# Forming the state weights of a chunked state-space scan in turned layout, from planes repeated over partitions

## The chip, the cores and the metric

The kernel runs on one core of a Trainium2 chip. The time is the device time of one execution in microseconds; times of several executions are given as their median. TensorE is called PE, VectorE DVE, ScalarE ACT, GpSimd POOL and SyncE SP, as in the profile.

## The reference

One hybrid decoder layer on 512 positions of width 1024, all in float32:

```
h    = rms_norm(x) * norm_w
proj = h @ w_in        # u_s, z_s (1024 each), q, k, v (1536 each), z_a (512), r_s, r_a (1024 each)
y_s  = s5(u_s) * silu(z_s) @ w_ssm_out
y_a  = dilated_attention(rope(qknorm(q)), rope(qknorm(k)), v) * silu(z_a) @ w_attn_out
out  = x + (sigmoid(r_s) * y_s + sigmoid(r_a) * y_a) @ w_o
```

The change lies in the S5 branch. It has 64 groups of 16 channels with 64 complex states each:

```
A    = exp(lam * exp(log_dt))                  # per group g and state n, complex
f    = (A - 1) / lam
bb   = f * (b_re + i b_im)                     # (g, n, q): q is one of 16 channels
h_t  = A * h_{t-1} + bb . u_t                  # a scan over 512 positions
y_t  = Re(c . h_t) + d * u_t, then GELU and a gated linear unit with w_glu
```

## The kernel before

The sequence is cut into 64 chunks of T = 8 positions. For each chunk the 8 inputs of a group enter the state at the chunk's end with the weights W[(k, q), n] = bb[n, q] A[n]^(7-k), a matrix with 128 rows (8 positions x 16 channels) for each group's 64 states, real and imaginary part. Groups are taken in pairs; unit j (0 to 7) has 8 groups, that is 4 pairs. The stages:

- **Projection.** cm_unit makes a 128-column block of the projection: 24 matmuls of 128x512 (three per 128 rows, since each float32 factor is split into a high and a low part). The weights come in by SP's queue (w_raw, two buffers), ACT makes the high part w_hi (L250), DVE the low part w_lo (L252); each has three buffers.
- **Constants.** DVE computes A and f on 64 partitions (one per group) in scr; pw holds A^1 to A^8 and f, made by doubling (L555 to L558). PE turns f (f_turn, "ftp") and the powers (a_turn, "atp") so that the states lie on partitions: fT and AT. POOL and DVE form BB = f b (L587 to L590).
- **W units.** w_unit(j) forms on DVE, by coef (L422 to L424), the products BB A^k with the states on partitions: six operations of 128x512. PE turns them by eight transposes of 128x128 ("wps") and ACT copies them out as W (L447), two buffers.
- **X units.** x_unit(j) multiplies W with u of all chunks on PE ("xps"); u has been stored to DRAM and loaded back with (position, channel) on partitions (ud, Uj, and sza in which early loads are kept). ACT puts the result into Xs.
- **Scan.** DVE runs the scan over the chunks on Xs (step, run_end, run_carry; L746 to L769), and each output chunk(j) then multiplies Xs and M on PE ("yps").

PE's order is written out by hand: each projection block has four slots, and the list events says at which slot a piece of the S5 work is put between the projection's matmuls. wx(j) stands at slot 16 + 3j and holds w_unit(j) and x_unit(j - 1); the first output chunk stands at slot 88. The orders of the other engines are set by a scheduler when the program is built, from data dependencies. SP's queue is served in order: a DMA that waits for a buffer holds up those behind it. A tile's tag names the memory that it shares in turn with others.

The tile names that the rows use: dd holds b (D1), BB and later M; ab holds the products of coef, later the coefficients of the outputs (ca); scn is the scan's work space; pj is a projection's PSUM tile; th a gate.

Of the kernel before, what the change touches and what calls it, by code (L numbers as in the profile page):

```python
# [20 lines left out]
P = 128  # L21
# [31 lines left out]
def tile_hybrid_block(ctx: ExitStack, tc: tile.TileContext, x, positions, norm_w, w_in, lam_re, lam_im,  # L53
# [3 lines left out]
    act, dve, pool, sp = nc.scalar, nc.vector, nc.gpsimd, nc.sync  # L57
# [50 lines left out]
    def bank(name):  # L108
        return ps_tile("g", name)
# [4 lines left out]
    def t2k(name, dtype=F32):  # L114
        return tmp.tile([P, 512], dtype, name=name, tag="t2k")
# [290 lines left out]
    def load_u(j, Uj=None):  # L406
        if Uj is None:
            Uj = t2k("Uj")
        sp.dma_start(Uj, ud[j].rearrange("q g s c -> s q g c"))
        return Uj.rearrange("p (g c) -> p g c", g=8)  # L410
# [3 lines left out]
    def coef(dst, p0, a1, a2, n0, n1, t, eng):  # L414

        n, ng = n1 - n0, dst.shape[1]
        sh = [P, ng, n, Q]
        gs = slice(p0, p0 + ng)
        ar = AT[:, 0, gs, n0:n1].unsqueeze(3).broadcast_to(sh)
        ai = AT[:, 1, gs, n0:n1].unsqueeze(3).broadcast_to(sh)  # L420
        tv = t[:, 0:ng * n * Q].rearrange("p (g k q) -> p g k q", g=ng, k=n)
        dve.tensor_tensor(dst, a1.unsqueeze(2).broadcast_to(sh), ar, op=ALU.mult)  # L422
        eng.tensor_tensor(tv, a2.unsqueeze(2).broadcast_to(sh), ai, op=ALU.mult)
        coefs[0] = dve.tensor_tensor(dst, dst, tv, op=ALU.add).ins  # L424
# [3 lines left out]
    def u_unit(j, at=(), ps=None):  # L428
# [5 lines left out]
                               ps.rearrange("p (r j i h) -> p r j i h", r=4, h=2, i=NI)).ins)  # L434
        sp.dma_start(ud[j].rearrange("q g s c -> g q (s c)"), uT)

    def w_unit(j):
        ba = ab[j % 2][:, 0:8 * T * Q].rearrange("p (a g k q) -> p a g k q", a=2, g=4, k=T)
        p4 = slice(4 * j, 4 * j + 4)
        for a in range(2):  # L440
            coef(ba[:, a], 4 * j, BB[:, 1 + a, p4], BB[:, a, p4], 1, T + 1, ab[2][:, 512 * a:], dve)
        W = big.tile([P, 8, P], F32, name="W", tag=("s6a", "s6b")[j % 2])
        for h in range(2):
            ps = bank("wps")
            for g in range(4):
                pe.transpose(ps[:, g * P:(g + 1) * P], ba[:, h, g].rearrange("p k q -> p (k q)"), ident)
            act.copy(W[:, 4 * h:4 * h + 4].rearrange("p g n -> p (g n)"), ps)  # L447
# [71 lines left out]
    mag = scr([G, N])  # L519
# [4 lines left out]
    sn = scr([G, N])  # L524
    cs = scr([G, N])
    sincos(sn, cs, th_, [G, N], "la")

    pw = big.tile([G, 2, 9, N], F32, name="pw", tag="s7a")
    dve.tensor_tensor(pw[:, 0, 0], mag, cs, op=ALU.mult)
    dve.tensor_tensor(pw[:, 1, 0], mag, sn, op=ALU.mult)  # L530
    den = scr([G, N])
    nr = scr([G, N])
    t1 = scr([G, N])
    t2 = scr([G, N])
# [12 lines left out]
    dve.tensor_tensor(pw[:, 1, 8], t1, den, op=ALU.mult)
    tq = big.tile([G, 2, 4, N], F32, name="tq", tag="s7b")
    for n in (1, 2, 4):

        br_ = pw[:, 0:1, n - 1:n, :].broadcast_to([G, 2, n, N])
        bi_ = pw[:, 1:2, n - 1:n, :].broadcast_to([G, 2, n, N])
        a = pw[:, :, 0:n, :]
        o = pw[:, :, n:2 * n, :]
        dve.tensor_tensor(o, a, br_, op=ALU.mult)  # L555
        dve.tensor_tensor(tq[:, :, 0:n], a, bi_, op=ALU.mult)
        dve.tensor_tensor(o[:, 0], o[:, 0], tq[:, 1, 0:n], op=ALU.subtract)
        dve.tensor_tensor(o[:, 1], o[:, 1], tq[:, 0, 0:n], op=ALU.add)  # L558
# [17 lines left out]
    abt = big.tile([P, 4096], F32, name="ab", tag="s5")  # L576
    ab = [abt[:, i * nca:(i + 1) * nca] for i in range(3)]
    fr, fi = (fT[:, i:i + 1, :].unsqueeze(3).broadcast_to([P, 2, H, Q]) for i in range(2))
    tb = ab[0][:, 0:1024].rearrange("p (a g q) -> p a g q", a=2, g=H)
    def f_turn():  # L580
        pf = bank("ftp")
        for i in range(2):
            for h in range(2):
                pe.matmul(pf[64 * h:64 * h + 64, i * H:(i + 1) * H], pw[:, i, 8], idg[:, h], start=True, stop=True,
                          skip_group_check=True)
        act.copy(fT.rearrange("p a g -> p (a g)"), pf[:, 0:2 * H])
        pool.tensor_tensor(tb, D1, fi, op=ALU.mult)  # L587
        dve.tensor_tensor(BB[:, 1:3], D1, fr, op=ALU.mult)
        dve.tensor_tensor(BB[:, 2], BB[:, 2], tb[:, 0], op=ALU.add)
        dve.tensor_tensor(BB[:, 1], BB[:, 1], tb[:, 1], op=ALU.subtract)  # L590
        act.activation(BB[:, 0], BB[:, 2], AF.Copy, scale=-1.0)

    def a_turn():
        ps = bank("atp")
        for i in range(2):
            for k in range(8):
                for h in range(2):
                    o = i * 8 * H + (7 - k) * H
                    pe.matmul(ps[64 * h:64 * h + 64, o:o + H], pw[:, i, k], idg[:, h], start=True, stop=True,
                              skip_group_check=True)  # L600
        for i in range(2):
            act.copy(AT[:, i, :, 0:8], ps[:, i * 8 * H:(i + 1) * 8 * H].rearrange("p (k g) -> p g k", k=8))
# [120 lines left out]
    H = G // 2  # L723
# [215 lines left out]
    events = [(3, begin_x), (6, lambda: early.update({3: load_u(3, sza[:, 3])})), (8, f_turn), (10, a_turn)]  # L939
# [309 lines left out]
    for c in range(KT):  # L1249
# [5 lines left out]
        ps = cm_unit(gT_hi, gT_lo, at=[(2, turn_wcol)] if c == 1 else ())  # L1255
# [82 lines left out]
    for cc in range(KT // 2):  # L1338
# [8 lines left out]
        for c2 in range(2):  # L1347
            c = 2 * cc + c2
# [47 lines left out]
```

## Time and profile before

| | |
|---|---|
| median of 3 runs | 678.64 us (677.83 to 680.23) |
| the profiled execution | 678.55 us, its span 676.5 us |
| granted PE clock | 1.00 |
| PE busy | 669.5 us (99%) |
| DVE busy | 465.3 us (69%) |
| ACT busy | 322.5 us (48%) |
| POOL busy | 118.2 us (17%) |

Busy time of an engine is the time in which at least one of its instructions runs. A row of a timeline has the start from the span's beginning, the duration, the engine, the line of the kernel, the operation, output and inputs and the tile; "x2" marks two such in a row, taken together. Durations of successive operations of one engine overlap a little, so starts are a better measure of what a row of them takes. The page's chain of work that ended last is followed back from the end, at each step to what released it. A window's row has from:to, its length, the busy time of the engine asked for (and its instructions), then the granted clock, the mean busy share of the 16 DMA engines and the GB/s that they moved; where no engine's busy time is shown, SP was asked for. A row of waits has who waited for whom, the sum in us, how many times, and the longest.

### The profile page before, as it was taken

How to read it: one execution, taken by the hardware profiler on the slowest of the kernel's cores; microseconds unless marked ns; L12 is line 12 of the kernel's file. 1: busy time of each engine (PE TensorE's matmuls, PEld its weight loads, DVE VectorE, ACT ScalarE, POOL GpSimd, SP SyncE). 2: the span in 40 equal slices, each digit the busy share in tenths (PEclk: the TensorE clock that was granted, in tenths of full speed). 3: DMA queues.
4: the chain of work that ended last, by engine and by line, in shares of the span. 5: the costliest groups of instructions: out<-in, count | busy, mean ns of one | idle time of the engine just before them, and what ended most of it. 6: DMA issues, size and time to landing. Idle time of an engine off the chain costs nothing.

```text
span 676.5 us, 12719 instructions
## 1 busy us (share of the span) xinstructions
PE 669.5 (99%) x4841; PEld 565.3 (84%) x4841; DVE 465.3 (69%) x964; ACT 322.5 (48%) x677; POOL 118.2 (17%) x274
## 2 busy tenths in 40 slices
PE   8999999999999999999999999999999999999997
PEld 7988888889888888878889888888888888888886
DVE  7989879999788365863238777658566856667531
ACT  6644552423467663431344674557456745633210
POOL 1020000600365329510000030012001200220000
PEclk9999999999999999999999999999999999999999
DMA  9665425552566543573332423222222213237231
GB/s 307 134 164 146 122 55 146 148 167 85 156 141 147 148 148 107 155 249 94 93 107 81 140 63 95 62 63 74 84 83 74 72 55 94 94 134 286 94 125 62
DMA packets 137380, 82.13 MB, mean 121 GB/s; under 512 B 32736, under 2 KB 125928, under 8 KB 137192
## 3 DMA queue, kind: packets, MB, share of 16 engines
q1 hardware_dynamic: 134968, 78.31, 39.2%
q0 software_dynamic: 2048, 2.36, 2.2%
q8 instruction: 38, 0.62, 0.4%
q10 hardware_dynamic: 304, 0.66, 0.3%
q14 instruction: 22, 0.18, 0.1%
HBM read 68.46 MB, written 10.49 MB: 117 GB/s over the span
## 4 chain that ended last, share of the span: by engine, by line
PE 92%; DVE 4%; issue 2%; ACT 1%; DMA 1%; POOL 0%; ACTq 0%; DVEq 0%; POOLq 0%
PE pj L69 76%; PE sps L69 3%; PE yps L69 2%; PE ot L69 2%; PE ptp L74 2%; PE qtp L74 2%; PE xps L69 1%; DVE gth L1258 1%; DVE w_lo L252 1%; PE wps L74 1%; ACT w_hi L250 1%; DMA x_all<-in_x_dram 1%; PE kps L69 1%; PE yT L74 1%; PE cps L69 0%
## 5 line engine op out<-in xcount | busy, mean ns | idle before, releaser
L250 ACT ACTIVATE w_hi<-w_raw 128x1024 fp32r<-128x1024 f32 x94 | 99.4, 1059 | 162.0 <-PE pj L69 132.2
L252 DVE TENSOR_TENSOR w_lo<-w_raw,w_hi 128x1024 fp32r<-128x1024 f32 x94 | 117.1, 1247 | 66.3 <-ACT w_hi L250 65.3
L69 PE MATMUL pj<-hT_hi,w_hi 128*128 128x512 f32 (+1 forms) x344 | 131.8, 385 | 0.0
L69 PE MATMUL pj<-hT_lo,w_hi 128*128 128x512 f32 (+1 forms) x344 | 128.8, 376 | 0.4 <-DVE hT_lo L355 0.4
L69 PE MATMUL pj<-hT_hi,w_lo 128*128 128x512 f32 (+1 forms) x344 | 126.8, 375 | 0.0
L69 PE MATMUL pj<-w_hi,hT_hi 128*128 128x512 f32 (+1 forms) x288 | 108.7, 377 | 0.0
L69 PE MATMUL pj<-w_hi,hT_lo 128*128 128x512 f32 (+1 forms) x288 | 105.6, 367 | 0.0
L69 PE MATMUL pj<-w_lo,hT_hi 128*128 128x512 f32 (+1 forms) x288 | 105.5, 366 | 0.0
L69 PEld LDWEIGHTS pj<-hT_hi,w_hi 128*128 128x128 f32 x344 | 64.7, 188 | 13.1 <-issue 1.3
L69 PEld LDWEIGHTS pj<-hT_lo,w_hi 128*128 128x128 f32 x344 | 64.8, 188 | 11.1 <-DVE hT_lo L355 0.6
L69 PEld LDWEIGHTS pj<-hT_hi,w_lo 128*128 128x128 f32 x344 | 63.7, 188 | 12.0
L69 PEld LDWEIGHTS pj<-w_hi,hT_lo 128*128 128x128 f32 x288 | 54.3, 189 | 9.1
L69 PEld LDWEIGHTS pj<-w_hi,hT_hi 128*128 128x128 f32 x288 | 54.4, 189 | 8.5 <-issue 0.5
L69 PEld LDWEIGHTS pj<-w_lo,hT_hi 128*128 128x128 f32 x288 | 54.5, 189 | 7.5
L1120 POOL COPY sw<-st 32x4 f32<-32x4 f32 x64 | 11.9, 185 | 175.0 <-ACT Pt L1076 172.2
L1021 DVE SCALAR_TENSOR_TENSOR qkp<-qtp,wcol,qkp 128x512 fp32r<-128x512 f32 (+1 forms) x32 | 23.6, 748 | 25.3 <-ACT qkp L1020 25.2
L1076 ACT ACTIVATE Pt<-Pt,st 128x256 f32<-128x256 f32 (+1 forms) x64 | 30.9, 484 | 19.8 <-DVE st L1074 19.8
L845 POOL DMA_DIRECT2D dd<-kt x64 | 33.8, 536 | 2.4 <-POOL kt L841 2.1
L1020 ACT ACTIVATE qkp<-qtp,wcol 128x512 fp32r<-128x512 f32 (+1 forms) x32 | 21.2, 683 | 23.0 <-PE qtp L74 20.8
L69 PE MATMUL pj<-w_lo,mT_hi 128*128 128x512 f32 (+1 forms) x72 | 26.3, 366 | 0.0
L69 PE MATMUL pj<-w_hi,mT_hi 128*128 128x512 f32 (+1 forms) x72 | 26.3, 366 | 0.0
L69 PE MATMUL pj<-w_hi,mT_lo 128*128 128x512 f32 (+1 forms) x72 | 26.3, 365 | 0.0
(301 smaller groups left out, 1189.6 us busy)
## 6 DMA issues: line engine op xcount, KB each, us to landing
w_raw<-in_w_in_dram SPq DMA_DIRECT2D x36, 512.0 KB
w_raw<-in_w_in_dram SPq DMA_DIRECT2D x112, 128.0 KB
w_raw<-in_w_glu_dram SPq DMA_DIRECT2D x8, 512.0 KB
w_raw<-in_w_ssm_out_dram SPq DMA_DIRECT2D x8, 512.0 KB
w_raw<-in_w_o_dram SPq DMA_DIRECT2D x8, 512.0 KB
w_early<-in_w_in_dram SPq DMA_DIRECT2D x4, 512.0 KB
ud<-uT SPq DMA_DIRECT2D x8, 256.0 KB
uss<-ud SPq DMA_DIRECT2D x8, 256.0 KB
```

The source lines that it names most:

```text
L69: last[0] = nc.tensor.matmul(*a, **k)
L74: last[0] = nc.tensor.transpose(*a, **k)
L250: last_act[0] = act.activation(hi, raw, AF.Copy).ins
L252: dve.tensor_tensor(lo, raw, hi.bitcast(F32), op=ALU.subtract)
L845: pool.dma_start(M[Q * t:Q * t + Q, :, 0:P - Q * t], kt[:, :, t:].rearrange("q g k p -> q g (k p)"))
L1020: act.activation(hi, ps[sl], AF.Copy, scale=w)
L1021: dve.scalar_tensor_tensor(lo, ps[sl], w, hi.bitcast(F32), op0=ALU.mult, op1=ALU.subtract)
L1076: act.activation(o, o, AF.Exp, bias=nm, scale=-1.0, accum_out=st[:, kind, 1, h, b:b + 1])
L1120: pool.tensor_copy(sw[32 * r:32 * r + 32, :, :, b], st[32 * b:32 * b + 32, 1, :, :, r])
L1258: dve.scalar_tensor_tensor(th, th, 1.0, z, op0=ALU.add, op1=ALU.mult)
```

## The change

The weights W are formed at once in the layout that x_unit needs, with (k, q) on partitions, so that PE need not turn them. For this the factors are laid out by DMA:

- **pf**: on 64 partitions (one per group) DVE forms f A^(7-k) for k = 0 to 7, from the powers A^1 to A^7 (three doublings, the last of three powers) and f. It is stored to DRAM as pfd.
- **btd**: b is turned once by eight transposes (b_turn, "btp", slot 4), copied by ACT and stored to DRAM by eight DMAs.
- **load_planes(j)**: four DMAs bring unit j's planes to 128 partitions x 512: pfd with each k's row repeated over the 16 channels, btd with each channel's row repeated over the 8 positions, real and imaginary part of each. Units 0 and 1 are loaded at slot 11; unit j + 2 is loaded when w_unit(j) has used its planes. The planes lie in ab's memory, two sets.
- **w_unit(j)**: the complex product of the planes, two multiplications of 128x1024, a subtraction and an addition of 128x512, written to W. No transposes, no copies by ACT.
- **f_turn** turns f and A; **a_powers** (slot 12) makes A^2 to A^8 on DVE from the turned A, with the states on partitions, in place of a_turn's 32 calls on PE. The copy of BB with its sign turned goes.

```diff
+    def load_planes(j):
+        PB = planes[j % 2].rearrange("p (a c) -> p a c", a=4)
+        for i in range(2):
+            p_, b_ = pfd[i, :, 8 * j], btd[i, :, 4 * j]
+            sp.dma_start(PB[:, i], bass.AP(p_.tensor, p_.offset, [(G * N, T), (0, Q), (1, 512)]))
+            sp.dma_start(PB[:, 2 + i], bass.AP(b_.tensor, b_.offset, [(0, T), (G * N, Q), (1, 512)]))
+        PBs[j] = PB
+
     def w_unit(j):
-        ba = ab[j % 2][:, 0:8 * T * Q].rearrange("p (a g k q) -> p a g k q", a=2, g=4, k=T)
-        p4 = slice(4 * j, 4 * j + 4)
-        for a in range(2):
-            coef(ba[:, a], 4 * j, BB[:, 1 + a, p4], BB[:, a, p4], 1, T + 1, ab[2][:, 512 * a:], dve)
+        PB = PBs.pop(j)
         W = big.tile([P, 8, P], F32, name="W", tag=("s6a", "s6b")[j % 2])
-        for h in range(2):
-            ps = bank("wps")
-            for g in range(4):
-                pe.transpose(ps[:, g * P:(g + 1) * P], ba[:, h, g].rearrange("p k q -> p (k q)"), ident)
-            act.copy(W[:, 4 * h:4 * h + 4].rearrange("p g n -> p (g n)"), ps)
+        Wv = W.rearrange("p (a m) n -> p a (m n)", a=2)
+        br, bi = (PB[:, 2 + i].unsqueeze(1).broadcast_to([P, 2, 512]) for i in range(2))
+        dve.tensor_tensor(Wv, PB[:, 0:2], br, op=ALU.mult)                      # L451
+        dve.tensor_tensor(PB[:, 0:2], PB[:, 0:2], bi, op=ALU.mult)              # L452
+        dve.tensor_tensor(Wv[:, 0], Wv[:, 0], PB[:, 1], op=ALU.subtract)        # L453
+        dve.tensor_tensor(Wv[:, 1], Wv[:, 1], PB[:, 0], op=ALU.add)             # L454
+        if j + 2 < 8:
+            load_planes(j + 2)
         return W
...
+    def times(o, a, br_, bi_, t):                                               # L562 to L565
+        dve.tensor_tensor(o, a, br_, op=ALU.mult)
+        dve.tensor_tensor(t, a, bi_, op=ALU.mult)
+        dve.tensor_tensor(o[:, 0], o[:, 0], t[:, 1], op=ALU.subtract)
+        dve.tensor_tensor(o[:, 1], o[:, 1], t[:, 0], op=ALU.add)
+
+    for n, m in ((1, 1), (2, 2), (4, 3)):
+        e = T - 1
+        sh = [G, 2, m, N]
+        times(pw[:, :, e - n - m:e - n], pw[:, :, e - m:e], ...)
+    sh = [G, 2, T - 1, N]
+    times(pf[:, :, 0:T - 1], pw[:, :, 0:T - 1], f1[:, 0:1]..., f1[:, 1:2]..., tq)
+    pfd = dram.tile([2, T, G, N], F32, name="pfd")
+    sp.dma_start(pfd.rearrange("a k g n -> g (a k) n"), pf.rearrange("g a k n -> g (a k) n"))
...
+    def b_turn():
+        bt = dd[:, 2048:3072].rearrange("p (a m c) -> p a m c", a=2, m=4)
+        for i in range(2):
+            ps = bank("btp")
+            for m in range(4):
+                pe.transpose(ps[:, m * P:(m + 1) * P], D1[:, i, 8 * m:8 * m + 8]..., ident)
+            act.copy(bt[:, i].rearrange("p m c -> p (m c)"), ps)
+            for m in range(4):
+                sp.dma_start(btd[i, :, 8 * m:8 * m + 8].rearrange("q m c -> m q c"), bt[:, i, m])
...
-    def a_turn():
-        ...                                    # 32 calls of pe.matmul into "atp", two copies to AT
+    def a_powers():
+        tv = t2k("tv")[:, 0:8 * H].rearrange("p (a g k) -> p a g k", a=2, g=H)
+        for n in (1, 2, 4):
+            sh = [P, 2, H, n]
+            times(AT[:, :, :, T - 2 * n:T - n], AT[:, :, :, T - n:T], ...)
...
-    events = [(3, begin_x), (6, ...), (8, f_turn), (10, a_turn)]
+    events = [(3, begin_x), (6, ...), (4, b_turn), (8, f_turn), (12, a_powers)]
+    events += [(11, lambda: load_planes(0)), (11, lambda: load_planes(1))]
```

On DVE, between the making of BB and the second X unit, the order before has the products of coef (L422 to L424, six per unit, all written to ab) with the low parts of weights between them:

```order
L422 TENSOR_TENSOR ab_518<-dd_513,AT_508 128x512 x4
L423 TENSOR_TENSOR ab_518<-dd_513,AT_508 128x512 x2
L252 TENSOR_TENSOR w_lo_692<-w_raw_689,w_hi_691 128x1024
L424 TENSOR_TENSOR ab_518<-ab_518 128x512 x2
```

On DVE at the same place now, W_748, W_775 and W_833 are the weights of units 0, 1 and 2, and ab holds the planes:

```order
L451 TENSOR_TENSOR W_748<-ab_525 128x1024
L451 TENSOR_TENSOR W_775<-ab_525 128x1024
L452 TENSOR_TENSOR ab_525<-ab_525 128x1024 x2
L453 TENSOR_TENSOR W_748<-W_748,ab_525 128x512
L454 TENSOR_TENSOR W_748<-W_748,ab_525 128x512
L252 TENSOR_TENSOR w_lo_744<-w_raw_741,w_hi_743 128x1024
L453 TENSOR_TENSOR W_775<-W_775,ab_525 128x512
L454 TENSOR_TENSOR W_775<-W_775,ab_525 128x512
L451 TENSOR_TENSOR W_833<-ab_525 128x1024
```

Units 0 and 1 run interleaved, and unit 2's first product, which needs new planes, follows the last of unit 1 at once.

On SP's queue, from the store of u's block 4 (uT_602) on, before:

```order
L435 DMA ud_336<-uT_602 8x16x512
L210 DMA w_raw_723<-in_w_in_dram 128x8x128
L435 DMA ud_336<-uT_686 8x16x512
L210 DMA w_raw_816<-in_w_in_dram 128x8x128
L435 DMA ud_336<-uT_720 8x16x512
```

On SP's queue from the store of the same block (uT_630 in the changed program) on, now:

```order
L435 DMA ud_336<-uT_630 8x16x512
L577 DMA pfd_513<-pf_480 64x16x64
L443 DMA ab_525<-btd_526 128x1x512 x4
L210 DMA w_raw_690<-in_w_in_dram 128x8x128
L442 DMA ab_525<-pfd_513 128x1x512 x4
L435 DMA ud_336<-uT_687 8x16x512
L210 DMA w_raw_741<-in_w_in_dram 128x8x128
L435 DMA ud_336<-uT_738 8x16x512
L210 DMA w_raw_814<-in_w_in_dram 128x8x128
L443 DMA ab_525<-btd_526 128x1x512 x4
L442 DMA ab_525<-pfd_513 128x1x512 x2
L210 DMA w_raw_878<-in_w_in_dram 128x8x128
```

The planes of units 0 and 1 (the first rows with ab) and then those of unit 2 stand between the weights and the stores of u; a plane that waits for DVE to finish with ab holds up the weights behind it. On PE the eight groups wps and the group atp are gone, the group btp stands at slot 4, and ftp has eight calls in place of four; the rest of PE's order is as before. From the first output chunks on, all engines have the order that they had.

More of the change, by code (lines that the diff above doesn't have):

```diff
@@ L526, in tile_hybrid_block @@
     sincos(sn, cs, th_, [G, N], "la")
-    pw = big.tile([G, 2, 9, N], F32, name="pw", tag="s7a")
-    dve.tensor_tensor(pw[:, 0, 0], mag, cs, op=ALU.mult)
-    dve.tensor_tensor(pw[:, 1, 0], mag, sn, op=ALU.mult)
+    pw = big.tile([G, 2, T, N], F32, name="pw", tag="s7a")
+    pf = big.tile([G, 2, T, N], F32, name="pf", tag="s7b")
+    a1 = pw[:, :, T - 2]
+    f1 = pf[:, :, T - 1]
+    dve.tensor_tensor(a1[:, 0], mag, cs, op=ALU.mult)
+    dve.tensor_tensor(a1[:, 1], mag, sn, op=ALU.mult)
     den = scr([G, N])
@@ L538, in tile_hybrid_block @@
     dve.reciprocal(den, den)
-    dve.tensor_scalar(nr, pw[:, 0, 0], -1.0, None, op0=ALU.add)
+    dve.tensor_scalar(nr, a1[:, 0], -1.0, None, op0=ALU.add)
     dve.tensor_tensor(t1, nr, lr, op=ALU.mult)
-    dve.tensor_tensor(t2, pw[:, 1, 0], li, op=ALU.mult)
+    dve.tensor_tensor(t2, a1[:, 1], li, op=ALU.mult)
     dve.tensor_tensor(t1, t1, t2, op=ALU.add)
-    dve.tensor_tensor(pw[:, 0, 8], t1, den, op=ALU.mult)
-    dve.tensor_tensor(t1, pw[:, 1, 0], lr, op=ALU.mult)
+    dve.tensor_tensor(f1[:, 0], t1, den, op=ALU.mult)
+    dve.tensor_tensor(t1, a1[:, 1], lr, op=ALU.mult)
     dve.tensor_tensor(t2, nr, li, op=ALU.mult)
     dve.tensor_tensor(t1, t1, t2, op=ALU.subtract)
[L547 to L558, printed above, removed]
+    dve.tensor_tensor(f1[:, 1], t1, den, op=ALU.mult)
+    def times(o, a, br_, bi_, t):
+        dve.tensor_tensor(o, a, br_, op=ALU.mult)
+        dve.tensor_tensor(t, a, bi_, op=ALU.mult)
+        dve.tensor_tensor(o[:, 0], o[:, 0], t[:, 1], op=ALU.subtract)
+        dve.tensor_tensor(o[:, 1], o[:, 1], t[:, 0], op=ALU.add)
+    tq = big.tile([G, 2, T - 1, N], F32, name="tq", tag="s6b")
+    for n, m in ((1, 1), (2, 2), (4, 3)):
+        e = T - 1
+        sh = [G, 2, m, N]
+        times(pw[:, :, e - n - m:e - n], pw[:, :, e - m:e], pw[:, 0:1, e - n:e - n + 1].broadcast_to(sh),
+              pw[:, 1:2, e - n:e - n + 1].broadcast_to(sh), tq[:, :, 0:m])
+    sh = [G, 2, T - 1, N]
+    times(pf[:, :, 0:T - 1], pw[:, :, 0:T - 1], f1[:, 0:1].unsqueeze(2).broadcast_to(sh),
+          f1[:, 1:2].unsqueeze(2).broadcast_to(sh), tq)
+    pfd = dram.tile([2, T, G, N], F32, name="pfd")
+    sp.dma_start(pfd.rearrange("a k g n -> g (a k) n"), pf.rearrange("g a k n -> g (a k) n"))
     H = G // 2
@@ L569, in tile_hybrid_block @@
     D1 = dd[:, 0:1024].rearrange("p (a g q) -> p a g q", a=2, g=H)
-    BB = dd[:, 2560:4096].rearrange("p (a g q) -> p a g q", a=3, g=H)
+    BB = dd[:, 3072:4096].rearrange("p (a g q) -> p a g q", a=2, g=H)
     bv = [b[0].rearrange("(m two) n q -> two n m q", two=2) for b in (b_re, b_im)]
@@ L578, in tile_hybrid_block @@
     fr, fi = (fT[:, i:i + 1, :].unsqueeze(3).broadcast_to([P, 2, H, Q]) for i in range(2))
-    tb = ab[0][:, 0:1024].rearrange("p (a g q) -> p a g q", a=2, g=H)
-    def f_turn():
[L581 to L586, printed above, removed]
-        pool.tensor_tensor(tb, D1, fi, op=ALU.mult)
[L588 to L591, printed above, removed]
@@ L593, in a_turn @@
-    def a_turn():
[L594 to L602, printed above, removed]
+    tb = dd[:, 1024:2048].rearrange("p (a g q) -> p a g q", a=2, g=H)
@@ new lines, in tile_hybrid_block @@
+    planes = [abt[:, i * 2048:(i + 1) * 2048] for i in range(2)]
+    PBs = {}
+    btd = dram.tile([2, Q, H, P], F32, name="btd")
+    def b_turn():
[3 more added lines that the diff above has]
+            for m in range(4):
+                pe.transpose(ps[:, m * P:(m + 1) * P], D1[:, i, 8 * m:8 * m + 8].rearrange("p g q -> p (g q)"), ident)
+            act.copy(bt[:, i].rearrange("p m c -> p (m c)"), ps)
+            for m in range(4):
+                sp.dma_start(btd[i, :, 8 * m:8 * m + 8].rearrange("q m c -> m q c"), bt[:, i, m])
@@ new lines, in f_turn @@
+    def f_turn():
+        pf_ = bank("ftp")
+        for i, t in enumerate((f1, a1)):
+            for a in range(2):
+                for h in range(2):
+                    o = (2 * i + a) * H
+                    pe.matmul(pf_[64 * h:64 * h + 64, o:o + H], t[:, a], idg[:, h], start=True, stop=True,
+                              skip_group_check=True)
+        act.copy(fT.rearrange("p a g -> p (a g)"), pf_[:, 0:2 * H])
+        act.copy(AT[:, :, :, T - 1], pf_[:, 2 * H:4 * H].rearrange("p (a g) -> p a g", a=2))
+        pool.tensor_tensor(tb, D1, fi, op=ALU.mult)
+        dve.tensor_tensor(BB, D1, fr, op=ALU.mult)
+        dve.tensor_tensor(BB[:, 1], BB[:, 1], tb[:, 0], op=ALU.add)
+        dve.tensor_tensor(BB[:, 0], BB[:, 0], tb[:, 1], op=ALU.subtract)
@@ L603, in a_turn @@
+    def a_powers():
+        tv = t2k("tv")[:, 0:8 * H].rearrange("p (a g k) -> p a g k", a=2, g=H)
+        for n in (1, 2, 4):
+            sh = [P, 2, H, n]
+            times(AT[:, :, :, T - 2 * n:T - n], AT[:, :, :, T - n:T], AT[:, 0:1, :, T - n:T - n + 1].broadcast_to(sh),
+                  AT[:, 1:2, :, T - n:T - n + 1].broadcast_to(sh), tv[:, :, :, 0:n])
         for i in range(2):
@@ L835, in m_unit @@
                     sl = slice(64 * h, 64 * h + 64)
-                    pe.matmul(ps[h][32 * m:32 * m + Q, 0:P], BB[sl, 1 + c, 4 * j + m, :], ca[sl, c, m, 1:9, :],
+                    pe.matmul(ps[h][32 * m:32 * m + Q, 0:P], BB[sl, c, 4 * j + m, :], ca[sl, c, m, 1:9, :],
                               start=c == 0, stop=c == 1, skip_group_check=True, tile_position=(64 * h, 32 * m))
@@ L937, in begin_x @@
         Xsv = Xs.rearrange("p a g i j -> p a g (i j)")
-    events = [(3, begin_x), (6, lambda: early.update({3: load_u(3, sza[:, 3])})), (8, f_turn), (10, a_turn)]
+    events = [(3, begin_x), (6, lambda: early.update({3: load_u(3, sza[:, 3])})), (4, b_turn), (8, f_turn), (12, a_powers)]
+    events += [(11, lambda: load_planes(0)), (11, lambda: load_planes(1))]
     events += [(W0 + 3 * j, lambda j=j: wx(j)) for j in range(8)] + [(W0 + 23, lambda: wx(8))]
```

## The prediction

> **What bounds the kernel now.** I read the page's busy shares first, then the chain that ended last, then the tile view of the transposes that the change removes.
>
> ```profile
> span 676.5 us, 12719 instructions
> PE 669.5 (99%) x4841; PEld 565.3 (84%) x4841; DVE 465.3 (69%) x964; ACT 322.5 (48%) x677; POOL 118.2 (17%) x274
> PE 92%; DVE 4%; issue 2%; ACT 1%; DMA 1%; POOL 0%; ACTq 0%; DVEq 0%; POOLq 0%
> ...
> 41.85 0.35 PE ftp L69 x8
> 45.15 1.99 PE atp L69 x64
> 55.53 0.87 PE wps L74 x8
> ...
> 61.39 1.08 PE xps L69 x32
> ...
> 99.42 0.87 PE wps L74 x8
> L74 PE MATMUL wps<-ident,ab x64: 270/272/273, 55.4 to 100.0; 128*128 128x128 f32 x64
> ```
>
> PE streams from end to end, and each group of transposes stands in that stream at its own price: 0.87 us for eight (wps, eight groups between 55 and 100 us), 1.99 for atp. What leaves PE shortens the run unless another engine becomes late. So the next view is DVE's timeline where its results are awaited: the scan over Xs, which must end before the first chunk of outputs reads Xs.
>
> ```profile
> 58.44 0.67 DVE L422 TENSOR_TENSOR ab<-dd,AT 128x512 f32<-128x512 f32 x1
> 59.04 1.21 DVE L252 TENSOR_TENSOR w_lo<-w_raw,w_hi 128x1024 fp32r<-128x1024 f32 x1
> 60.18 0.67 DVE L423 TENSOR_TENSOR ab<-dd,AT 128x512 f32<-128x512 f32 x1
> ...
> 111.83 1.22 DVE L746 TENSOR_TENSOR scn<-Xs,scn 128x1024 f32<-128x1024 f32 x1
> ...
> 174.62 0.69 DVE L751 TENSOR_TENSOR Xs<-Xs,scn 128x512 f32<-128x512 f32 x1
> 175.53 1.10 PE L69 MATMUL yps<-dd,uss 128*64 128x64 f32 x32
> 176.56 1.16 PE L69 MATMUL yps<-ab,Xs 64*64 64x64 f32 x64
> 39.54:111.83 72.29, 63.02 (x93) 1.00 0.46 120
> 111.83:175.31 63.48, 60.37 (x97) 1.00 0.50 145
> DVE w_lo L252 <- ACT w_hi L250: 7.0, 10, 1.5
> DVE ab L422 <- PE wps L74: 2.4, 3, 1.0
> DVE sza L630 <- ACT th L629: 0.7, 1, 0.7
> DVE ab L422 <- ACT AT L602: 0.4, 1, 0.4
> ```
>
> The scan's last step ends at 174.62 + 0.69 = 175.31, and PE first needs it at 176.56: a slack of 1.25 us. In the two windows (second number: DVE's busy time) DVE works 123.4 of 135.8 us. The four rows of its waits, taken over 39 to 176 us, add to 10.5 us, and each is a wait on PE or on ACT behind PE. So DVE is second to PE here, by very little. The starts also give DVE's real prices back to back: 0.60 us for 512 columns (58.44 to 59.04), 1.14 for 1024 (59.04 to 60.18).
>
> **The change part by part.**
>
> PE, removed: 8 x 0.87 = 7.0 for wps and 1.99 for atp, 9.0 us. Added: eight transposes btp, the same kind, 0.87, and four more calls ftp, 0.35 x 0.7 = 0.25 (the group of eight records holds a fixed part). Net 7.9 us, and nothing else on PE changes. If all of it counted, PE would read Xs at 176.56 - 7.9 = 168.7.
>
> ACT loses sixteen copies of W and one negation, and its two copies of A become one; it gains two copies of 512 columns. It is 48% busy, so I book nothing for it except that DVE no longer waits for wps (2.4) or AT (0.4).
>
> DVE, rows for the new work:
>
> ```profile
> 37.06 0.41 DVE L555 TENSOR_TENSOR pw<-pw 64x256 f32<-64x256 f32 x1
> 37.40 0.41 DVE L556 TENSOR_TENSOR tq<-pw 64x256 f32<-64x256 f32 x1
> ...
> 39.54 0.67 DVE L555 TENSOR_TENSOR pw<-pw 64x512 f32<-64x512 f32 x1
> 40.14 0.68 DVE L556 TENSOR_TENSOR tq<-pw 64x512 f32<-64x512 f32 x1
> ...
> 43.95 2.96 DVE L588 TENSOR_TENSOR dd<-dd,fT 128x1024 f32<-128x1024 f32 x1
> 47.01 0.69 DVE L589 TENSOR_TENSOR dd<-dd,ab 128x512 f32<-128x512 f32 x1
> ...
> 140.11 0.41 DVE L761 TENSOR_TENSOR scn<-scn 128x128 f32<-128x128 f32 x1
> ```
>
> Prices by start: 0.34 for 256 columns, 0.60 for 512, so about 0.07 + columns/960.
> - The W units: 48 operations of 512 x 0.60 = 28.8 go; 8 x (2 x 1.14 + 2 x 0.60) = 27.8 come. -1.0.
> - The last power step shrinks from four powers to three: 2 x 0.60 + 2 x 0.34 becomes 2 x 0.47 + 2 x 0.27. -0.4.
> - The products f A^k are new: two operations of 896 columns at 1.0, two of 448 at 0.53. +3.1.
> - The powers of A in the state's layout, twelve operations of 32 to 256 columns: 2.2 by the line above, up to 3.5 if nine-strided columns cost what the strided L761 does (0.41 for 128). I take 2.5.
>
> Sum +4.2 us of DVE work ahead of the scan's end. So with every attributed wait gone the scan could end at 175.31 + 4.2 - 10.5 = 169.0, hardly after PE's 168.7; any wait that is left or new moves it later, one for one. That is the sum that decides.
>
> [...]
>
> New waits: the planes. Each unit now reads four planes of 256 KB that SP's queue brings.
>
> ```profile
> 26.64 0.70 SPq L435 DMA_DIRECT2D ud<-uT  x1
> 31.43 0.61 SPq L409 DMA_DIRECT2D sza<-ud  x1
> ...
> 45.74 1.24 SPq L435 DMA_DIRECT2D ud<-uT  x1
> 47.03 0.45 SPq L210 DMA_DIRECT2D w_raw<-in_w_in_dram  x1
> SPq L409 <- DMA ud<-uT: 11.8, 4, 4.0
> DMA to landing us min/median/max: 1.6/3.4/5.6
> 42.00:44.00 2.00, 1.00 0.96 245
> 57.00:70.00 13.00, 1.00 0.56 135
> 70.00:85.00 15.00, 1.00 0.49 132
> 85.00:100.00 15.00, 1.00 0.18 51
> 610.00:615.00 5.00, 1.00 0.94 387
> ```
>
> Issuing costs SP about 0.45 us each. Writing 256 KB to DRAM and being allowed to read it took 26.64 + 0.70 to 31.43, 4.1 us. The landing row is the one view with landings (copies into dd from POOL's queue); its median 3.4 is the nearest row for a plane, its ends 1.6 and 5.6 are my bounds.
> - First planes. DVE: 39.54 + 1.6 (last powers, one f) + 3.1 = 44.2 for the products; weights' low part 1.14, the scaled B 3.06 (43.95 to 47.01, stretched by POOL beside it, as before) and 1.2, powers 2.5, another low part 1.14: DVE is ready for W at 53.3. The planes: pfd goes out behind u4's store, at 45.7 as that does now, may be read 4.1 later, 49.8; two reads issued at 50.8, landed at 54.2. Wait 0.9, say 1. W of unit 0 is whole at 54.2 + 4 x 1.14 + 1.2 = 60.0 (two units interleave). PE wants it at 61.39 - 1.99 - 1.75 + 1.12 = 58.8, so PE stands 1.2 us. That is not added: PE would wait at the scan anyway.
> - Unit 2's planes overwrite unit 0's, whose last reader ends at 60.0. SP first issues four btd reads, then the two pfd reads at 61.5; landed 64.9. DVE is there at 60.0 + 1.14 + 1.2 = 62.3. Wait 2.6 (0.8 to 4.8 by the bounds). It cannot be below nothing.
> - Units 3 to 7: between the end of unit j and the start of j + 2 lie one unit (3.5), a low part (1.14) and a gate (0.6 in most): 4.6 to 5.2 us, against 0.9 + 3.4 = 4.3. Hidden by 0.3 to 0.9 us; bounds nothing and 1.5 us each.
> - Of the 7.7 us of waits for w_hi and th, DVE now being late leaves about 1.0.
>
> New and left waits 1.0 + 2.6 + 1.0 = 4.6: scan ends 173.6. PE's Xs matmuls then start at 173.6 and not 176.56: 3.0 us earlier. Behind it the orders of all engines are the same as now and PE keeps streaming, so 3.0 us stays.
>
> DMA volume is covered: 8 x 1.05 MB at 387 GB/s (a window of long rows) is 2.7 us of all engines per unit, beside a share of 0.56 to 0.18 now; SP's 41 extra issues are 18 us in some 55 in which SP mostly waits. If that cover were gone, weights would be late next, not planes alone.
>
> [...]
>
> **Sum.** The profiled execution took 678.55 us, 2.05 more than its span, and stands 0.09 under the median of 678.64. 678.55 - 3.0 = 675.5.
>
> **Rivals.** A measurement of this kernel can tell about 0.3%, 2.0 us: below 676.6 is faster, above 680.7 slower.
> - B, PE's whole saving: the planes land near 1.6 us, so unit 2's wait falls to 0.8 and the first goes. Scan end 169.0 + 0.8 + 0.5 or so; 678.55 - 7.5 = 671. For it: the fixed part of DVE is fitted on the pessimistic side for the powers. Against: every conversion would have to be there in time.
> - C, no measurable change: what is gained is spent on first planes 2 us later, or on units 3 to 7 each waiting 0.4 us. Scan end about 175.6, 677.5. For it: the slack of units 3 to 7 is only 0.3 to 0.9.
> - D, slower: the planes' round trip becomes the period. With a landing of L the extra over the sum is 2(L - 3.4) for units 0 and 2 and 5(L - 4.1) for units 3 to 7 (middle slack). It eats the 3.0 at L = 4.4; at the row's maximum, 5.6, it is 11.9: scan end 185.5, 687.5. At L = 5, 7.7: 683.2. For it: in 42 to 44 us the DMA engines are at 0.96 with 245 GB/s, at which a unit's planes alone take 4.3 us, and weights and planes share SP's one queue in order. Against: 387 GB/s for long rows, and the share is half free from 57 us on.
>
> **How the numbers follow.** My forecast (waits 3 to 6.5 us, 674 to 677.5) 0.50; B 0.13; C 0.22; D 0.15, likeliest near 683. Faster: 0.45 of the first and B, 0.58. Same: the rest of the first, C and 0.02 of D, 0.29. Slower: 0.13. The range 671 to 680 leaves out most of D and the lower half of B, under 2 in 10.
>
> **What would show it.** In the profile after: no wps and atp, btp near 0.87; L451 and L452 at 1.21, L453 and L454 at 0.67; DVE waiting some 2.6 us for DMA ab at the third W; PE waiting for DVE ahead of the first xps and ahead of yps from Xs (at 173 to 174, no slack). B shows as the scan ending by 170; D as DVE waiting for ab at every unit and SP's weights late. The forecast is wrong if plane landings are not near 3.4 us, or if the powers in AT cost well over 3.5.

## The result and the profile after

The changed kernel takes 722.76 us (median of four runs, 722.55 to 723.27) against 678.63 (677.83 to 680.23): a ratio of 1.0648, 95% interval 1.0628 to 1.0668. It is 44.1 us slower; the forecast was 675.5. The profiled execution took 722.87 us.

The page of the changed kernel: span, busy times, and by 40 slices PE, the clock that PE was granted, and the DMA engines.

```profile
span 720.6 us, 12560 instructions
PE 671.2 (93%) x4729; PEld 564.2 (78%) x4729; DVE 469.3 (65%) x964; ACT 314.3 (44%) x661; POOL 118.9 (16%) x274
PE   8992758799969999999999999999999999999998
PEclk9997888899997999999999999999999999999999
DMA  9557556456442674446433342322313222237331
```

The same rows of the kernel before:

```profile
PE   8999999999999999999999999999999999999997
PEclk9999999999999999999999999999999999999999
```

PE, at 9 from slice 1 to slice 38 before, has holes from slice 3 to slice 7, which is 54 to 144 us, and one at slice 11, 198 to 216 us. Its clock drops in slices 3 to 7 too, and in slice 12, behind the second hole. PE's waits, and DVE's between 44 us and the scan's end (total us, times, longest):

```profile
PE xps L69 <- DVE W L453: 33.5, 4, 14.8
PE yps L69 <- DVE Xs L783: 8.2, 1, 8.2
```
```profile
DVE W L451 <- DMA ab<-pfd: 27.1, 6, 11.2
DVE w_lo L252 <- ACT w_hi L250: 13.5, 7, 11.4
DVE W L451 <- PE pj L69: 4.7, 1, 4.7
```

PE waits for W and for the scan; DVE waits for planes, for weights and, once, for PE. Against 10.5 us of waits before there are 45.3. DVE's window from 44 us to the scan's end, of before and then of after (length, busy time with instructions in brackets, PE's clock, DMA share, GB/s):

```profile
44.00:175.31 131.31, 120.11 (x183) 1.00 0.47 130
```
```profile
44.00:217.49 173.49, 126.05 (x182) 0.90 0.55 159
70.00:100.00 30.00, 16.33 (x19) 0.89 0.58 176
```

DVE's work grew by 5.9 us and its idle time from 11.2 to 47.4: together the scan ends 42.2 us later. PE's first read of Xs moved from 176.56 to 217.55:

```profile
217.55 1.99 PE L69 MATMUL yps<-ab,Xs 64*64 64x64 f32 x64 [8.15 <-DVE Xs L783]
```

That is 41.0 us of 44.3 between the two profiled executions. The same 64 matmuls took 1.16 us before and take 1.99 here, and those behind them 0.63 instead of 0.39: the clock granted to PE is 0.50 from 217.5 to 223.2 us and 1.00 from 224 to 228.

What the planes do is seen in the chain that ended last, in SP's queue, and on ACT and DVE (the trace has no landing row for loads that SP issues):

```profile
98.51 6.70 DMA ab<-pfd
107.53 7.50 DMA ab<-pfd
119.56 9.37 DMA ab<-pfd
```
```profile
41.57 4.92 SPq L611 DMA_DIRECT2D btd<-dd  x8
...
48.63 0.62 SPq L577 DMA_DIRECT2D pfd<-pf  x1
49.30 4.17 SPq L443 DMA_DIRECT2D ab<-btd  x4
53.52 0.63 SPq L210 DMA_DIRECT2D w_raw<-in_w_in_dram  x1
54.25 6.36 SPq L442 DMA_DIRECT2D ab<-pfd  x4
```
```profile
63.07 1.06 ACT L250 ACTIVATE w_hi<-w_raw 128x1024 fp32r<-128x1024 f32 x1 [12.98 <-DMA w_raw<-in_w_in_dram]
64.16 1.23 DVE L252 TENSOR_TENSOR w_lo<-w_raw,w_hi 128x1024 fp32r<-128x1024 f32 x1 [11.37 <-ACT w_hi L250]
66.61 1.23 DVE L451 TENSOR_TENSOR W<-ab 128x1024 f32<-128x1024 f32 x1 [1.22 <-DMA ab<-pfd]
```

The three plane loads on the chain took 6.70, 7.50 and 9.37 us from the end of their issue, and not 3.4. A weights load that in the kernel before went out at 41.04 us goes out at 53.52, behind eight stores of turned b, the store of pf and four plane loads, and ACT gets it only at 63.07; with it the low part of those weights comes at 64.16 on DVE, and the first W stands behind it. Yet the DMA engines are busy only 0.58 of the time between 70 and 100 us. That was the riddle: late transfers with four tenths of the engines' time free.

### The profile page after: what moved, and what is told of

Its sections match the earlier page's. It is cut to its first block, busy times and chain, and to the rows that moved or that the text cites. A ratio compares the mean times of both kernels' runs of the same rounds, so it can differ in the third digit from the quotient of the medians.

```text
span 720.6 us, 12560 instructions
## 1 busy us (share of the span) xinstructions
PE 671.2 (93%) x4729; PEld 564.2 (78%) x4729; DVE 469.3 (65%) x964; ACT 314.3 (44%) x661; POOL 118.9 (16%) x274
## 4 chain that ended last, share of the span: by engine, by line
PE 68%; issue 11%; DMA 7%; DVE 5%; POOL 4%; SPq 3%; ACT 1%; DVEq 0%; POOLq 0%; ACTq 0%
PE pj L69 58%; DMA ab<-pfd 3%; POOL dd L877 3%; PE sps L69 2%; PE ot L69 2%; PE ptp L74 2%; SPq L442 2%; PE qtp L74 1%; DMA ud<-uT 1%; SPq L443 1%; DMA Uj<-ud 1%; DVE w_lo L252 1%; DMA x_all<-in_x_dram 1%; POOL kt L873 1%; DVE ab L452 1%
## 5 line engine op out<-in xcount | busy, mean ns | idle before, releaser
L250 ACT ACTIVATE w_hi<-w_raw 128x1024 fp32r<-128x1024 f32 x94 | 99.4, 1058 | 187.3 <-PE pj L69 125.6
L69 PE MATMUL pj<-hT_hi,w_hi 128*128 128x512 f32 (+1 forms) x344 | 133.6, 390 | 0.0
L1054 DVE SCALAR_TENSOR_TENSOR qkp<-qtp,wcol,qkp 128x512 fp32r<-128x512 f32 (+1 forms) x32 | 23.6, 748 | 25.0 <-ACT qkp L1053 24.9
L873 POOL TENSOR_TENSOR kt<-kt,dg 16x128 f32<-16x128 f32 x8 | 6.3, 793 | 172.0 <-ACT kt L872 172.0
L451 DVE TENSOR_TENSOR W<-ab 128x1024 f32<-128x1024 f32 x8 | 9.8, 1225 | 31.9 <-DMA ab<-pfd 27.1
```

The lines of the kernel that those rows point to most:

```text
L69: last[0] = nc.tensor.matmul(*a, **k)
L250: last_act[0] = act.activation(hi, raw, AF.Copy).ins
L451: dve.tensor_tensor(Wv, PB[:, 0:2], br, op=ALU.mult)
L1054: dve.scalar_tensor_tensor(lo, ps[sl], w, hi.bitcast(F32), op0=ALU.mult, op1=ALU.subtract)
```

## The experiments

**Theory.** The access patterns of the planes have eight rows as slowest dimension, and my guess was that such a transfer keeps only half of the 16 DMA engines busy. Rivals: reading the same few DRAM rows from many partitions at once is slow (hot rows); SP's one queue in order issues too late (queue); more bytes than the engines carry (volume).

**The shapes by themselves.** Six phases of 16 loads of 256 KB, without the kernel. The access patterns on DRAM's side, `ld` being a row's length: (0) `[(ld,128)]`, (1) `[(0,8),(ld,16)]`, (2) `[(128ld,8),(0,16)]`, (3) `[(ld,16),(0,8)]`, (4) `[(0,16),(128ld,8)]`, (5) `[(128ld,8),(ld,16)]`. In fact fifteen loads of each phase were issued one behind the other at the start, in this order, and the sixteenth of each later.

> Not the kernel: six phases by themselves, each of 16 loads of 256 KB from the input weights into 128 partitions by 2 KB, with nothing of the reference computed. Phases in order: (0) 128 distinct rows; (1) 8 outermost and adjacent rows, 16 rows within; (2) as the changed kernel's pf planes: 8 rows, each repeated 16 times within; (3) 16 rows outermost, each repeated 8 times within; (4) 16 repetitions outermost of 8 rows; (5) distinct rows, 8 outermost far apart. The phases each move 4.19 MB on the side that writes. Eight-engine theory: phases 0, 3 and 4 run all engines and take about 11 to 13 us (4.19 MB at 330 to 390 GB/s); 1 (if its two dimensions don't fold into one), 2 and 5 run at a DMA share of at most 0.50 and take about twice that, 22 to 25 us. Hot-row theory: 2, 3 and 4 are slow together, and 0, 1 and 5 fast. Queue theory: all six alike.

Windows within phase 0, phases 1 and 2, phases 3 and 4, and phase 5, placed by the bytes of each phase (length, PE's clock, DMA share, GB/s):

```profile
13.00:22.00 9.00, 1.00 1.01 356
24.00:52.00 28.00, 1.00 0.53 203
68.00:84.00 16.00, 1.00 1.05 268
96.00:112.00 16.00, 1.00 0.53 203
```

With eight outermost, repeated (1, 2) or not (5), the share is 0.53 and 203 GB/s, and stays there with the queue full. With 16 outermost, each row repeated (3, 4), it is 1.05 and 268 GB/s, with 128 distinct rows (0) 1.01 and 356. Other outermost dimensions, and 16 distinct rows, were not run, so how much of the quarter between 356 and 268 GB/s is the repetition is not shown.

**The shapes in the kernel.** Three edits of the changed kernel.

```diff
 # e1_copies_outermost (and u's copy in DRAM as [8, Q, T, 8, C], so that its loads are 128 rows of 2 KB)
-... bass.AP(p_.tensor, p_.offset, [(G * N, T), (0, Q), (1, 512)])
-... bass.AP(b_.tensor, b_.offset, [(0, T), (G * N, Q), (1, 512)])
+... bass.AP(p_.tensor, p_.offset, [(0, Q), (G * N, T), (1, 512)])
+... bass.AP(b_.tensor, b_.offset, [(G * N, Q), (0, T), (1, 512)])
 # e2_distinct_rows: both planes from w_in, [(128 * 9216, T), (9216, Q), (1, 512)]
 # e3_one_row: both planes [(0, P), (1, 512)]
```

> Change: every plane is read with the 16 lanes outermost on the DRAM side (the 16-way repetition, or the 16 rows, is the slow dimension, not the 8), and the copy of u in DRAM is laid out so that its loads are 128 plain rows of 2 KB. The bytes, the repetition 16-fold and 8-fold, the queue and the order of the work stay. Eight-engine theory (the plane loads, the stores of u and its loads run on half of the 16 DMA engines because their slowest dimension is 8): the DMA share in 48 to 128 us rises above 0.59 or ends earlier, the planes land in about 4 us instead of 6.7 to 9.4, W's waits for planes (27.1 us of DVE before the scan's end in the changed kernel) fall under 8, and the time comes to 675 to 690 us. Hot-row theory (128 partitions read the same few DRAM rows at the same time, and that is slow whatever the engines): planes still 6.7 to 9.4 us, time 715 to 725. Queue theory (SP's in-order queue issues too late behind instructions that take 4 to 7 us): 705 to 725.

> Change: each plane is loaded from 128 different rows of 2 KB of the input weights, so nothing is repeated, in an access of the same shape as the changed kernel's (8 by 16 by 512, 8 outermost), so W is not the reference's. Eight-engine theory: as slow as the changed kernel, 715 to 725 us, planes 6.5 to 9.5 us. Hot-row theory: planes in about 3.4 to 4 us, 675 to 690 us. Queue theory: 715 to 725.

> Change: each plane is one single DRAM row of 2 KB repeated to all 128 partitions, the strongest repetition there is, in an access whose slowest dimension is 128; W is not the reference's. Eight-engine theory: planes on all 16 engines, landing in about 4 us, 680 to 695 us (u's stores and loads stay on 8 engines). Hot-row theory: planes slower than 6.7 us, 720 us or more. Queue theory: 715 to 725.

With the lanes outermost the kernel takes 701.01 us (four runs), 1.032 of before (1.0295 to 1.0344): 21.8 us of the 44.1 went with the eight outermost. One row to all 128 partitions, the most repetition possible, takes 702.26 with u's transfers as they were, so the planes' shape alone is enough, and hot rows are not what cost these 21.8 us. It is a single run, and not like e1 in all else: DVE waits 17.5 us for planes in it and 8.6 in e1, and in the slices of its page from 70 to 105 us the DMA engines are at 0.7 and 0.8, where those of e1 show 0.9 twice. Why the two still end within 1.3 us was not taken apart. The distinct rows with eight outermost take 713.88, and DVE still waits 17.7 us for planes before the scan's end. These planes don't depend on pf: SP issues them from 41.4 us, and the making of pf moves to a later place on DVE, so the orders differ and this number settles little by itself. But 701 is not the 675 to 690 that I expected, and the plane loads on the chain did not get shorter. Of the run with the lanes outermost: the plane loads on the chain that ended last, two of DVE's waits, and two windows:

```profile
48.88 6.99 DMA ab<-btd
80.12 8.83 DMA ab<-btd
89.01 6.63 DMA ab<-pfd
95.67 7.79 DMA ab<-pfd
```
```profile
DVE w_lo L252 <- ACT w_hi L250: 13.4, 6, 8.6
DVE W L451 <- DMA ab<-pfd: 8.6, 2, 6.7
```
```profile
44.00:195.19 151.19, 125.41 (x182) 0.93 0.66 179
70.00:100.00 30.00, 18.42 (x21) 0.84 0.95 247
```

The engines are now at 0.95 and 247 GB/s from 70 to 100 us, and by my estimate a plane waits for those ahead of it. A control, the kernel before with the new layout of u alone (two lines):

> Change to the kernel before: only the new layout of u's copy in DRAM (its loads are 128 plain rows of 2 KB on 16 engines, its stores 256 B pieces). No theory gives it a large effect, since nothing waits for u in the kernel before: 676 to 681 us.

678.88 us, no effect.

**The volume.** Of the run with the lanes outermost, planes left out:

```diff
 # e6_no_planes: units 2 to 7 load nothing
-        if j + 2 < 8:
-            load_planes(j + 2)
+        PBs[j + 2] = PB
 # e18_half_planes: units 2 to 7 load pf's two planes only
+            if j < 2:
                 sp.dma_start(PB[:, 2 + i], ...)
```

> Change to the kernel with the lanes outermost: only units 0 and 1 load planes; units 2 to 7 multiply what stands in the buffers, so their W is wrong and 24 of 32 plane loads (6.3 MB) are gone, all else being as it was. Volume theory: DMA share in 70 to 105 us falls under 0.5, the second stall and the late scan go, only the first stall (weights behind the planes of units 0 and 1, about 9 us) is left: 678 to 688 us. If VectorE's own work made the scan late: 693 to 702 us.

> The kernel with the lanes outermost, in which units 2 to 7 load only their two planes of pf; the two of b are those of units 0 and 1, so W is wrong there. 12 of 32 plane loads (3.1 MB) are gone. Volume theory: the scan ends between 184.5 us (no planes after unit 1) and 195.2 us (all planes), near the middle or lower, and the time is 689 to 696 us. Round-trip theory (each unit still waits for its two planes of pf, issued when its buffer comes free): scan's end 193 to 196 us, 698 to 702 us.

688.52 and 688.71 us. Half of the volume gives back all that the whole gives. The same window, first with no planes, then with half:

```profile
70.00:100.00 30.00, 26.39 (x30) 0.96 0.42 127
```
```profile
70.00:100.00 30.00, 23.44 (x26) 0.95 0.83 214
```

By these three volumes (701.01 with all, 688.71 with half, 688.52 us with none) it is a threshold, not a price per byte. In a unit the engines bring 1.05 MB of planes, 0.39 of weights (a unit takes three of the four slots of a projection block, whose weights are 0.52) and 0.26 of u; at 247 GB/s that is 6.9 us. With half of the planes it is 4.8. Unstalled, PE's X matmuls of two units stand 5.4 us apart (76.22 and 81.63 us in the run with the lanes outermost). By this estimate the supply sets the pace at 6.9 us a unit and not at 4.8. The rows agree: on DVE, from unit 2 to unit 7, the first products of W come 6.8 us apart with all planes (74.83 to 108.80 us) and 5.9 with none (68.92 to 98.53); with half, PE is busy without a break from 70 to 110 us, and the projection blocks of the chain that ended last begin 5.4 to 6.0 us apart (76.94 to 105.14). The round-trip theory, as it was put, is out: DVE still waits for two planes (7.1 us in three waits), and the time loses nothing by it. One rival is left without a run: by the shapes alone repeated rows come at 268 GB/s and distinct ones at 356, so a part of the volume's price may be the repetition.

**The queues.** Planes issued by POOL instead of SP (e5), the nine stores as well (e9), and that without planes from unit 2 on (e12):

```diff
 # e5: in load_planes, on top of e1
-            sp.dma_start(PB[:, ...
+            pool.dma_start(PB[:, ...
 # e9: also
-    sp.dma_start(pfd..., pf...)      ...      sp.dma_start(btd[i, ...], bt[:, i, m])
+    pool.dma_start(pfd..., pf...)    ...      pool.dma_start(btd[i, ...], bt[:, i, m])
 # e12: e9 with the edit of e6
```

> Change to the kernel with the lanes outermost (701.0 us): the plane loads are issued from POOL's queue instead of SP's, so that the loads of the projection weights, which SP issues in order, no longer stand behind them. Volume theory (with all 16 engines in use, the planes' 8.4 MB and the weights, u's stores and loads fill them: share 0.88 to 0.98 from 50 to 100 us at about 250 GB/s): the weights come earlier and the planes later, the first stall of 9.4 us shrinks, the planes' waits grow, and the time stays within 690 to 702 us. Queue theory (only the order on SP's queue delays the weights): no stall left, 672 to 685 us.

> Change to the kernel with the planes on POOL's queue (698.7 us; there the weights load that stood at 41.0 us in the kernel before was issued at 51.7, behind eight stores of turned b and the store of pf): those nine stores go to POOL's queue too, so that nothing of the round trip stands ahead of the weights. If the first stall (8.75 us) is the weights' place in SP's order: weights issued at about 41 to 44 us, the stall under 2 us, and the time 683 to 692 us (the planes' volume still makes stalls later). If the weights wait for full DMA engines wherever they stand: stall 6 us or more and 694 to 700 us.

> The run with all round trips on POOL's queue, without the plane loads of units 2 to 7 (W is wrong for these). If weights queued behind the stores (first stall) and the planes' volume are together all of the loss, this comes to 670 to 677 us, under the kernel before, since 7.9 us of PE's work are gone; if VectorE's chain to the scan's end is late for another reason, 679 us or more with a wait of PE for the scan's end.

698.73, 700.62 and 689.99 us. The first is within what volume allows, though its first stall hardly shrank (8.75 us after 9.36). In the other two what I had hoped for did not come: e9 kept its stall and ended 0.6 us above the slower of its two ranges, and e12 kept a wait of 5.4 us for the scan's end. Of planes that POOL issues the trace has the landings, here in e5, with the lanes outermost (minimum, median, maximum from issue):

```profile
DMA to landing us min/median/max: 4.3/7.0/9.1
```

With the stores on POOL the weights were indeed early (SP issued them at 39.15 and 45.74), but the first stall stayed at 8.07 us. POOL's queue in e9 shows why:

```profile
45.24 3.40 POOL L623 TENSOR_TENSOR dd<-dd,fT 128x1024 f32<-128x1024 f32 x1
48.59 0.88 POOL L577 DMA_DIRECT2D pfd<-pf  x1
...
50.50 1.90 POOL L936 MEMSET dd<- 128x1024 f32 x2
...
54.59 2.17 POOL L442 DMA_DIRECT2D ab<-pfd  x4
```

pf was complete at 44.57 us and its store went out at 48.59, behind a product; the planes went out at 54.59, behind memsets. The first stall had changed hands, from weights behind planes on SP to planes behind POOL's own work.

**The places in PE's order.** `W0` and `Y0` say at which place of the projections the W units and the outputs stand.

```diff
-    W0, K0B, V0B, Y0 = 16, 49, 74, 88
+    W0, K0B, V0B, Y0 = 16, 49, 74, 91      # e7 (on e5), e10 (on e9)
+    W0, K0B, V0B, Y0 = 20, 49, 74, 91      # e13 (on e9), e15 (on e12)
+    W0, K0B, V0B, Y0 = 20, 49, 74, 98      # e14 (on e9), chunks 8/3 places apart instead of 11/3
```

> Change to the kernel with the planes on POOL's queue: the chunks' outputs start three places later in PE's order (91 instead of 88, some 4.7 us of other projections ahead of them), so that PE has that work left while VectorE ends the scan. If what is left of the loss is PE's wait for the scan's end, the time falls by up to 4.7 us against the run with POOL's queue alone; if it is stalls ahead of the scan, by under 1 us.

> The same, and the chunks' outputs three places (some 4.7 us of PE's work) later, 91 instead of 88. If a wait of PE for the scan's end is left in the run with all round trips on POOL's queue, it falls by up to 4.7 us, and the time with it; with POOL's queue for the loads alone this was worth 4.7 us (694.1 against 698.7).

> The same two shifts with all planes loaded (the run with all round trips on POOL's queue: 700.6 us; with the outputs alone later 692.3). If the chain planes, W, scan sets the end: the first stall of 8 us goes, PE comes that much earlier to the outputs and waits there for the scan instead, 686 to 693 us. If PE's place for the first unit sets it: 680 to 685 us.

> W units four places later, outputs ten places later (98) and closer together (8/3 places for a chunk instead of 11/3), all planes loaded. If the chain planes, W, scan ends at about 190 us whatever PE does, PE's wait for it falls by another 7 places (11 us), less what the closer chunks cost: 676 to 686 us. If the chunks then wait for VectorE's coefficients instead: 686 to 695 us.

> The run without the planes of units 2 to 7 (690.0 us, first stall 8.9 us, wait of 5.4 us for the scan's end), with the W units four places (some 6.3 us of PE's work) later in PE's order, 20 instead of 16, and the outputs three later, 91 instead of 88; W is wrong for units 2 to 7. If the round trip to the first unit and the planes' volume are all of the loss: no stall over 1 us left on PE, granted clock 1.0, 671 to 676 us, the 7.9 us of PE's saving in full or nearly. If something else holds the scan: 679 us or more.

694.07, 692.29, 692.90, 688.57 and 687.27 us. Three places were worth the 4.7 us on e5, and 8.3 on e9, more than the work put there. These are single runs; in e10 the wait for the scan is 1.7 us instead of 5.7, and the 64 matmuls behind it take 1.16 us instead of 1.98. e13 fits the chain planes, W, scan: the first stall halved (4.1 us), the wait for the scan came back (5.7), the time stayed. The last was to be a floor and is none: ACT waited 7.8 us for weights while the planes of units 0 and 1 were being loaded, and `W0` also moves the coefficients and the steps of the scan, which are placed relative to it, so that the scan began at 124.2 us. In e14 PE waits no more for the scan, and the stalls at the W units are left (8.6 us in four). No version here beats the kernel before.

**All runs on one line.** DVE from 44 us to the scan's end, from the same view as above:

| run | DVE busy | idle | scan's end | time of that execution | time minus scan's end |
|---|---|---|---|---|---|
| before | 120.1 | 11.2 | 175.3 | 678.6 | 503.2 |
| after | 126.1 | 47.4 | 217.5 | 722.9 | 505.4 |
| e1, lanes outermost | 125.4 | 25.8 | 195.2 | 702.2 | 507.0 |
| e2, distinct rows | 135.0 | 31.1 | 210.1 | 713.9 | 503.8 |
| e3, one row | 125.1 | 28.0 | 197.1 | 702.3 | 505.2 |
| e5, planes by POOL | 126.0 | 23.2 | 193.2 | 698.7 | 505.5 |
| e9, stores too | 125.3 | 23.5 | 192.8 | 700.6 | 507.9 |
| e12, no planes | 125.9 | 15.6 | 185.5 | 690.0 | 504.5 |
| e6, no planes | 126.0 | 14.4 | 184.5 | 688.5 | 504.1 |
| e18, half | 125.1 | 16.7 | 185.8 | 688.7 | 502.9 |
| e7, e10, e13, e15: outputs at 91 | 125.6 to 126.1 | 16.5 to 23.9 | 186.2 to 194.1 | 687.3 to 694.1 | 499.3 to 501.9 |
| e14: outputs at 98 | 125.9 | 24.9 | 194.8 | 688.6 | 493.8 |

With the outputs at 88 the time is the scan's end plus 503 to 508 us, whatever stalls lie ahead on PE. The scan's end is 44 us plus the two columns, by construction. All changed kernels but e2, where the making of pf fell into the window, have the same DVE work; what differs is DVE's idle time.

## Why the prediction was wrong

- **PE's saving** was right as a count (4729 matmuls instead of 4841). With half of the planes PE is busy 665.4 us instead of 669.5, a slow stretch behind the first stall included.
- **DVE as the engine that decides, one for one,** was right: the table above.
- **DVE's work, +4.2 us:** the rows came as forecast (L451 at 1.22, L453 at 0.68, pf complete at 44.48 against 44.2). The window from 44 us shows +5.9, but about 1.9 of it are a low part of weights and a coefficient's product that had stood outside the window, and most of the products f A^k lie ahead of it, so the two figures don't compare term by term. The powers of A were the term that was off: 4.9 us by their starts (46.67 to the last one's end at 52.80, less 1.2 for two other operations) instead of 2.5. That is over the 3.5 that the prediction named as a sign of being wrong. Their first operation took 2.01 us while a product ran on POOL (44.71 to 48.55 us); in the kernel before, the scaled B beside a product on POOL had taken 2.96, now it took 1.21 beside one. So that POOL stretches DVE's work, as the prediction has it, is not shown. All this is small beside the 36.2 us by which DVE's idle time grew.
- **The step that failed is the sentence that the DMA volume is covered,** "2.7 us of all engines per unit" at 387 GB/s. I priced planes with a window of long rows and never asked what share of the engines this shape keeps busy. By itself it is 0.53: 203 GB/s, 5.2 us per unit, with u's stores and loads to come. With 16 outermost it is 268 GB/s by itself and 247 in e1 with all else, and there planes, weights and u together take 6.9 us per unit where PE allows 5.4. In the changed kernel units 2 to 7 come 9.0 us apart on DVE (83.89 to 129.12); at 203 GB/s planes and u alone are 6.5 of it, and the rest, with the engines' share at 0.43 between 85 and 90 us, was not taken apart. The sum asked whether each plane is back in time, and never whether the engines can bring everything in a unit's time.
- **The landing of 3.4 us** was taken from POOL's copies into dd, which are 8 to 64 KB each and not 256. On the chain it was 6.70 to 9.37, over my upper bound of 5.6; in e5, where the trace has the landings, the median is 7.0. With the engines at 0.95, as in e1, a plane by my estimate also waits for those ahead of it, and a row of small copies has no price for that.
- **The first planes.** I had W of unit 0 begin at 54.2 us; it began at 66.61, because the weights' low part stands ahead of it on DVE and the weights were behind the round trip on SP. The prediction named that ("weights would be late next") and gave it no number. In e6 and e18 the scan ends 9.2 and 10.5 us later than before: 5.9 and 5.0 of these are DVE's work, and 3.2 and 5.5 more idle time, in which the late weights are the longest wait (6.6 and 7.2 us).
- **Rival D had the mechanism:** the planes' round trip becomes the period, and its two signs came, waits for planes (six) and late weights. With L = 7.5, the middle one of the three on the chain, its formula gives 2 x 4.1 + 5 x 3.4 = 25.2 us, 701 us, still 22 short, since it holds neither the late weights nor the clock. A chance of 0.15 and a cap at 5.6 us for L were the error of judgement.
- **Missed altogether:** PE's clock, 0.97 over the profiled execution and not 1.00 as before. PE's busy time rose by 1.7 us although 7.9 us of work left, so by this estimate about 9.6 us went to lower clock behind its stalls.

What stays open: whether a version with late enough places, all weights ahead of the planes and half of the bytes would beat the kernel before. None was built that computes the reference with half of the bytes. The bound is near: with no idle time at all from 44 us, DVE's 125 to 126 us end the scan at 169 to 170, 5 to 6 us before the 175.3 of the kernel before.

## What to carry to other kernels

Before a transfer is called hidden, read its access pattern for the slowest dimension (here the repeated rows came at 203 GB/s with eight outermost and at 268 with sixteen), price it at the rate measured for its shape, and add up all that the queues must bring in one period, not only the new transfer's own landing. Where a second engine stands close behind the first, look at its idle time up to the point where its result is awaited; here that one number gave the time of every run that left the outputs at their place. Work that is moved from PE to DMA enters a queue, and what stands behind it there can be the next to be late, as the weights were here (out at 53.52 us and not 41.04).

## What the hardware showed that I had not expected

- With eight outermost, repeated and distinct rows came at the same 203 GB/s, at a share of 0.53; at a share of 1.01 to 1.05, rows repeated with 16 outermost came at 268 and 128 distinct ones at 356 GB/s.
- A stall of PE costs more than its length. Of the run with the lanes outermost:

```profile
67.76 2.37 PE L69 MATMUL xps<-sza,W 128*64 128x64 f32 x32 [9.36 <-DVE W L453]
76.22 1.15 PE L69 MATMUL xps<-sza,W 128*64 128x64 f32 x32
95.09 2.37 PE L69 MATMUL xps<-Uj,W 128*64 128x64 f32 x32 [2.62 <-DVE W L453]
```

  The same 32 matmuls take 2.37 us behind a stall and 1.15 otherwise, and the slow stretch, in which matmuls of the projection take 0.63 instead of 0.39 us, lasts some 6 us (67.76 to 74.05). A stall of 2.62 us already shows it. Length alone does not decide here: in e7 a stall of 2.46 us is followed by matmuls at 0.40 and the clock from 80 to 90 us is 1.00, while in e10 the stretch from 110 to 120 us, in which PE is idle for 2.28, shows a clock of 0.83. What else decides was not shown.
